# Score blocks of a head packed into fewer PSUM banks, and the projection tiles of the next heads dealt out one by one, in a one-core encoder block on Trainium2

## The chip, the cores and the metric

The kernel runs as one program on one core of a Trainium2 chip. TensorE (PE) multiplies matrices, VectorE (DVE) and ScalarE (ACT) read its results and work on tiles, GpSimd (POOL) takes element-wise work between SBUF tiles, and SyncE (SP) issues most DMAs. PE writes into PSUM, which this kernel uses as eight banks of 128 x 512 fp32; everything else lives in SBUF. The metric is the device time of one execution, in microseconds (us), lower is better. Before the change the median of three runs is 889.13 us (888.93 to 891.29).

## The reference, cut to what matters

One layer over 512 frames of 1024 features, batch 1. What the change touches is the attention branch:

```python
u = einsum('bsd,de->bse', rmsnorm(h, norm_mix_g), w_in)       # q | k | v | rnn_x | rnn_gate | gate_A | gate_B
ya = chunked_band_attention(q, k, v, rel_table) @ w_attn_out  # 16 heads x 64, chunks of 64, key band of 9 chunks
yb = (rg_lru(causal_depthwise_conv(xr)) * gelu(gr)) @ w_rnn_out
h  = h + (sigmoid(ga) * ya + sigmoid(gb) * yb) @ w_o
h  = h + (silu(g) * up) @ w_ffn_out                           # FFN of 2816, on rmsnorm(h)
return rmsnorm(h, final_norm_g)
```

With 512 frames the band is just the causal mask by chunks, so a head has four query blocks of 128 rows whose scores are 128, 256, 384 and 512 keys wide.

## The kernel before, in words

All weights and activations are fp32 and are split into a high and a low part (`split`, L78: ACT copies the high part, DVE subtracts it to get the low part); a product is three matmuls, high x high, high x low and low x high (`mm3`, L72). The profile therefore names PE work by L74, L75 and L76, which are the lines of that helper, and splits by L80 (ACT) and L81 (DVE).

The stages, in order of time: normalise and transpose x; the RNN branch's projections, gates and scan; the products with `w_rnn_out` (`po_yb`); 16 attention heads; the products with `w_attn_out` (`po_ya`), `w_o`, then the FFN and the final norm. The attention stage is the one that the change rewrites.

Within it PE's order is written out by hand (`manual_schedule` for PE, L720): the loop of L721 emits for each head h

1. `transposed(h)` (L660): ten 128 x 128 transposes of the normalised probabilities `p` into three PSUM tiles `pT`, the third of them of the `mm` kind; each is split by ACT and DVE into `pp`;
2. `scores(h+1)` (L638): for each of the four query blocks two matmuls (L650, L651) into a PSUM tile `s`; then DVE adds the bias and takes the row maximum (L653, the maximum is called `m`), ACT takes the exponential (L654), DVE the reciprocal `rl` of the row sums (L655) and POOL multiplies (L657, four pieces a head);
3. the tiles that `laid(h)` (L700) puts before the product: projections that later heads need. `q_tile` and `k_tile` (L593, L604) make queries and keys of a pair of heads, 24 matmuls of 512 columns each; `v_tile` (L627) makes values of four heads for 128 frames, 24 matmuls of 256 columns; in the last four heads `gate` (L560) makes gate tiles `po_ga`;
4. `weigh(h)` (L677): the product `o` with the values, eight matmuls;
5. the tiles that `laid(h)` puts behind it.

The order of the other engines' instructions is made by a scheduler from the same program.

PSUM is dealt out by tags (L69): four banks `mm`, two `s`, two `t`. In this stage `t` belongs to the first two tiles of `pT`, `s` to the scores of query blocks 0 and 1, and `mm` to everything else: the third `pT`, the scores of blocks 2 and 3, every q, k, v and gate tile, and `o`. A PE matmul that opens a tile waits until the readers of the bank's last tile are done.

The copies of a k tile are many (L604): for each of its two heads ACT writes the high part (L611), DVE the low part (L612), ACT copies the high part to the other half of the partitions (L613), and POOL copies the low part there (L614).

Weights come through `prefetch` (L217) in the order of `plan` (L94): SP loads a `raw` tile (three buffers), ACT and DVE split it into `whl` (four buffers). `weights(name)` loads ahead by one planned chunk. The tiles `rnn` and, later, `aT` (the attention output, split) share four large buffers of the tag `big`.

Of the kernel before, what the change touches and what calls it, by code (L numbers as in the profile page):

```python
# [36 lines left out]
def block_kernel(ctx: ExitStack, tc: tile.TileContext, x, norm_mix_g, w_in, b_merge, rel_table,  # L37
# [23 lines left out]
    z_stack, zp = opened("z", 1, "right")  # L61
# [7 lines left out]
    def mm_tile(name, tag="mm"):  # L69
        return ps.tile([P, S], F32, tag=tag, bufs=4 if tag == "mm" else 2, name=name)  # L70
# [37 lines left out]
    def plan_v(gr):  # L108
        plan(f"v{gr}", cols(w_in, C_V + gr * CW))
# [4 lines left out]
        plan(f"yb{j}", cols(w_rnn_out, j * P))  # L114
    for pr in range(1, HEADS // 2):
        plan_qk(pr)
        if pr in (2, 4, 6):
            plan_v(pr // 2)
    for j in (4, 6):
        plan(f"ga{j}", cols(w_in, C_GA + j * P))  # L120
    for j in range(0, KT, 2):
# [11 lines left out]
    whole, every = slice(0, CW), slice(0, S)  # L133
    raws = {}
    extra = {}

    def load(name, k):
        _, parts, rows, kts = chunks[index[name]]
# [78 lines left out]
    def prefetch(n):  # L217
        while len(made) < min(n, len(chunks), index.get(barrier[0], len(chunks))):
            name, parts, rows, kts = chunks[len(made)]
            if name in strassen:  # L220
                made.append(weight_sums(name))
                continue
            tiles = []
            wide = sum(width for *_, width in parts)
            step = 4 * CW // wide
            for k in range(0, kts, step):
                n_ = min(step, kts - k)
                if name in extra:
                    hl = extra[name].tile([P, 2, n_, wide], F32R, tag="whl", bufs=4, name=f"whl_{name}_{k}")
                else:  # L230
                    hl = wp.tile([P, 2, n_, wide], F32R, tag="whl", bufs=4, name=f"whl_{name}_{k}")
                if (name, k) not in raws:
                    load(name, k)
                raw = raws.pop((name, k))
                if len(made) == 0 and k:
                    act.activation(hl[:, 0], raw[:], AF.Copy)
                    pool.tensor_sub(hl[:, 1], raw[:], f(hl[:, 0]))
                else:
                    split(hl[:, 0], hl[:, 1], raw[:])
                tiles.append(hl)  # L240
            made.append(lambda part, k, at, tiles=tiles, step=step: tiles[k // step][:, part, k % step, at])
# [312 lines left out]
        return po  # L554


    zs = [[zp.tile([P, 2, S], F32, name=f"z{w}{j}") for j in range(0, KT, 2)] for w in "ab"]
    ta, zB = ([t[j // 2][:, j % 2] for j in range(KT)] for t in zs)

    def gate(w, j):  # L560
        po = tile_of(f"g{'ab'[w]}{j - j % 2}", j % 2)
        act.activation((ta, zB)[w][j], po[:], AF.Tanh, bias=hb[:, 16 + 8 * w + j:17 + 8 * w + j], scale=0.5)
# [30 lines left out]
    def q_tile(pr):  # L593
        po = mm_tile(f"po_q{pr}")
        project(po, weights(f"qk{pr}"), 0, xnT)
        q = qk_pool(pr).tile([P, 2, S], F32R, tag="qk", bufs=3, name=f"q{pr}")
        for e in range(2):
            own, other = halves(e)
            src = backwards(po[own, :])
            act.activation(blocks(q[own, e]), src, AF.Copy, scale=0.125)  # L600
            dve.scalar_tensor_tensor(blocks(q[other, e]), src, 0.125, blocks(f(q[own, e])), ALU.mult, ALU.subtract)
        qk[pr] = [q]

    def k_tile(pr):  # L604
        po = mm_tile(f"po_k{pr}")
        project(po, weights(f"qk{pr}"), 1, xnT)
        kh = qk_pool(pr).tile([P, 2, S], F32R, tag="qk", bufs=3, name=f"kh{pr}")
        kl = qk_pool(pr).tile([P, 2, S], F32R, tag="qk", bufs=3, name=f"kl{pr}")
        for e in range(2):
            own, other = halves(e)  # L610
            act.activation(kh[own, e], po[own, :], AF.Copy)  # L611
            dve.tensor_sub(kl[own, e], po[own, :], f(kh[own, e]))  # L612
            act.activation(kh[other, e], po[own, :], AF.Copy)  # L613
            pool.tensor_copy(kl[other, e], kl[own, e])  # L614
        qk[pr] += [kh, kl]
# [11 lines left out]
    def v_tile(gr, t):  # L627
        wv = weights(f"v{gr}")
        po = mm_tile(f"po_v{gr}_{t}", "mm" if gr else "t")
        for k in range(KT):  # L630
            mm3(po[:, 0:256], xnT[k][:, 0, t * P:(t + 1) * P], xnT[k][:, 1, t * P:(t + 1) * P],
                wv(0, k, whole), wv(1, k, whole), k == 0, k == KT - 1)
        v = aw.tile([P, 2, 4, HD], F32R, tag="v", bufs=8, name=f"v{gr}_{t}")
        split(v[:, :, 0::3], v[:, :, 1:3], po[:, 0:256].rearrange("p (a b d) -> p a b d", a=2, b=2))
        vs.setdefault(gr, []).append(v)


    def scores(h):  # L638
        pr, e = divmod(h, 2)
        q, kh, kl = qk[pr]  # L640
        bias = bias_tile(h)
        lsum = cp.tile([P, NT], F32, tag="lsum", bufs=2, name=f"l{h}")
        nmax = cp.tile([P, NT], F32, tag="nmax", bufs=2, name=f"m{h}")
        rl = cp.tile([P, NT], F32, tag="rl", bufs=2, name=f"rl{h}")
        prob = [aw2.tile([P, (qb + 1) * P], F32, tag=f"p{qb}", name=f"p{h}_{qb}") for qb in range(NT)]
        for qb in range(NT):
            w = (qb + 1) * P
            sc = mm_tile(f"s{h}_{qb}") if qb >= 2 else ps.tile([P, S], F32, tag="s", bufs=2, name=f"s{h}_{qb}")
            qs = q[:, e, qb * P:(qb + 1) * P]
            pe.matmul(sc[:, 0:w], qs, kh[:, e, 0:w], start=True, stop=False)  # L650
            pe.matmul(sc[:, 0:w], qs, kl[:, e, 0:w], start=False, stop=True)  # L651

            dve.tensor_tensor_reduce(prob[qb][:], sc[:, 0:w], bias[:, S - w:S], -1.0, 3e38, ALU.add, ALU.min, nmax[:, qb:qb + 1])  # L653
            act.activation(prob[qb][:], prob[qb][:], AF.Exp, bias=nmax[:, qb:qb + 1], scale=-1.0, accum_out=lsum[:, qb:qb + 1])  # L654
        dve.reciprocal(rl[:], lsum[:])  # L655
        for qb in range(NT):
            pool.tensor_scalar(prob[qb][:], prob[qb][:], rl[:, qb:qb + 1], 1.0, ALU.mult, ALU.mult)  # L657
        return prob
# [39 lines left out]


    def laid(h):  # L700
        m, at = divmod(h, 4)
        qs, ks, va = (lambda pr: lambda: q_tile(pr)), (lambda pr: lambda: k_tile(pr)), (lambda t: lambda: v_tile(m + 1, t))
        if h >= 12:
            return [lambda: gate(0, h - 8)], []
        first_, second = 2 * m + 2, 2 * m + 3
        return {0: (([qs(1), ks(1)] if m == 0 else []) + ([] if m == 0 else [qs(first_)]), [qs(first_)] if m == 0 else []),
                1: ([ks(first_)], [va(0)]),
                2: ([va(1), va(2)], [va(3)]),
                3: ([qs(second)], [ks(second)])}[at]

    for t in range(NT):
        v_tile(0, t)
# [274 lines left out]
```

## Time and profile before

| what | value |
|---|---|
| median of three runs | 889.13 us |
| the three runs | 889.13, 891.29, 888.93 us |
| span of the profiled execution, first to last instruction | 887.1 us |
| PE busy in the span | 870.7 us, 98% |
| DVE busy in the span | 551.2 us, 62% |
| ACT busy in the span | 470.8 us, 53% |
| POOL busy in the span | 105.3 us, 12% |
| attention stage, first transpose to first `po_ya` | 247.53 to 443.93 us |
| PE busy from 247 to 444 us | 191.60 of 197.00 us |

The profiled execution's own time is known only as its span, 887.1 us; the median of the runs lies 2.0 us above it, which is what lies around the first and the last instruction.

How to read it: a busy engine is one with an instruction running, and matmuls overlap, so PE's busy share alone does not tell where it loses time. The useful view in this kernel is the list of PE instructions in order of time: the distance from one start to the next is what a matmul costs the stream, and a longer distance is a wait. A bracket at the end of such a row gives the idle time before it and the instruction that ended it. "<-" reads "out from in" when it stands between tiles and "waited for" when it stands between instructions.

### The profile page before, as it was taken

Reading aid. Unit: us, or ns where it says so; the run is one execution under the profiler, and the core shown is the slowest. Engines: PE = TensorE matmul, PEld = TensorE weight load, DVE = VectorE, ACT = ScalarE, POOL = GpSimd, SP = SyncE. Lnnn points to the kernel's source line nnn. Section 1 sums busy time; section 2 is a strip of 40 time slices with the busy share of each in tenths; the row PEclk is TensorE's granted clock in tenths of the full one; section 3 lists DMA queues with packets and bytes.
Section 4 is the critical chain, followed back from the end, with each engine's and each line's share of the span. In section 5 each row is a group of like instructions: output and inputs, shape, how many; then the busy total and the mean of one; then the engine's idle time right before and its main releaser. Section 6 shows DMA issues by size and latency. Waiting matters only on the chain.

```text
span 887.1 us, 13322 instructions
## 1 busy us (share of the span) xinstructions
PE 870.7 (98%) x5220; PEld 775.2 (87%) x5220; DVE 551.2 (62%) x856; ACT 470.8 (53%) x823; POOL 105.3 (12%) x141
## 2 busy tenths in 40 slices
PE   8999999999999999999999999999999999999997
PEld 5988888888888889797888889999999999888886
DVE  6776557563456576675556556888878887553203
ACT  7566646652256575666633465656555555723103
POOL 4012111120112131212200000000000001300100
PEclk9999999999999999999999999999999999999999
DMA  8323223333333232232123720524333332353002
GB/s 266 90 77 110 82 94 95 120 95 95 107 91 88 81 98 73 72 108 72 48 96 117 263 67 30 162 77 123 116 95 96 99 126 86 120 181 123 28 1 96
DMA packets 86080, 90.11 MB, mean 102 GB/s; under 512 B 5376, under 2 KB 74608, under 8 KB 86016
## 3 DMA queue, kind: packets, MB, share of 16 engines
q1 hardware_dynamic: 84640, 85.78, 31.0%
q10 hardware_dynamic: 1376, 3.47, 1.0%
q8 instruction: 41, 0.67, 0.3%
q14 instruction: 23, 0.19, 0.1%
HBM read 87.10 MB, written 2.14 MB: 101 GB/s over the span
## 4 chain that ended last, share of the span: by engine, by line
PE 95%; DVE 2%; ACT 1%; DMA 1%; issue 0%; ACTq 0%; DVEq 0%
PE po_out L75 5%; PE po_out L76 5%; PE po_out L74 5%; PE p_fg L74 2%; PE o L688 2%; PE p_fg L76 2%; PE p_fu L76 2%; PE p_fu L75 2%; PE p_fg L75 2%; PE p_fu L74 2%; PE po_v L74 2%; PE po_ga L74 2%; PE po_v L76 2%; PE po_v L75 2%; PE po_q L74 2%; PE po_k L74 2%
## 5 line engine op out<-in xcount | busy, mean ns | idle before, releaser
L75 PE MATMUL po_out<-whl_fo,act_hi 128*128 128x512 f32 (+1 forms) x198 | 72.5, 366 | 0.0
L74 PE MATMUL po_out<-whl_fo,act_hi 128*128 128x512 f32 (+1 forms) x198 | 72.3, 366 | 0.0
L76 PE MATMUL po_out<-whl_fo,act_lo 128*128 128x512 f32 (+1 forms) x198 | 71.7, 365 | 0.0
L81 DVE TENSOR_TENSOR whl_fo<-raw_fo,whl_fo 128x1024 fp32r<-128x1024 f32 x22 | 27.8, 1273 | 44.3 <-ACT whl_fo L80 43.7
L657 POOL TENSOR_SCALAR p<-p,rl 128x128 f32<-128x128 f32 (+1 forms) x64 | 35.8, 577 | 138.6 <-DVE rl L655 138.3
L871 POOL TENSOR_TENSOR act_lo<-act,act_hi 128x1024 fp32r<-128x1024 f32 x4 | 10.9, 2718 | 323.9 <-ACT act_hi L870 321.9
L80 ACT ACTIVATE whl_fo<-raw_fo 128x1024 fp32r<-128x1024 f32 x22 | 23.0, 1057 | 49.0 <-PE po_out L76 35.2
L74 PEld LDWEIGHTS po_out<-whl_fo,act_hi 128*128 128x128 f32 x198 | 37.4, 189 | 6.0
L75 PEld LDWEIGHTS po_out<-whl_fo,act_hi 128*128 128x128 f32 x198 | 37.4, 189 | 6.0
L76 PEld LDWEIGHTS po_out<-whl_fo,act_lo 128*128 128x128 f32 x198 | 37.3, 189 | 5.9
L654 ACT ACTIVATE p<-p,m 128x128 f32<-128x128 f32 (+1 forms) x64 | 35.8, 562 | 11.1 <-DVE m L653 10.7
L74 PE MATMUL po_v<-whl_v,xnT 128*128 128x256 f32 x128 | 36.5, 285 | 0.0
L76 PE MATMUL po_v<-whl_v,xnT 128*128 128x256 f32 x128 | 36.2, 283 | 0.0
L75 PE MATMUL po_v<-whl_v,xnT 128*128 128x256 f32 x128 | 36.2, 283 | 0.0
L653 DVE CUSTOM_DVE_ANT_0 p<-s,bias 128x128 f32<-128x128 f32 (+1 forms) x64 | 29.7, 484 | 0.7 <-issue 0.5
L81 DVE TENSOR_TENSOR whl_qk<-raw_qk,whl_qk 128x1024 fp32r<-128x1024 f32 x16 | 20.9, 1308 | 14.3 <-ACT whl_qk L80 14.3
L75 PE MATMUL po_xr<-xnT,whl_xr 128*128 128x512 f32 (+1 forms) x80 | 27.9, 354 | 0.6 <-DVE xnT L358 0.5
L74 PE MATMUL po_q<-xnT,whl_qk 128*128 128x512 f32 x64 | 25.3, 395 | 2.7 <-DVE m L653 2.7
L81 DVE TENSOR_TENSOR whl_fg_s<-s_fg,whl_fg_s 128x1024 fp32r<-128x1024 f32 x20 | 25.6, 1294 | 3.7 <-ACT whl_fg_s L80 3.7
L81 DVE TENSOR_TENSOR pp<-pT,pp 128x384 fp32r<-128x384 f32 (+1 forms) x48 | 27.9, 596 | 0.0
L74 PE MATMUL po_gr<-xnT,whl_gr 128*128 128x512 f32 (+1 forms) x80 | 27.8, 349 | 0.1
L76 PE MATMUL po_gr<-xnT,whl_gr 128*128 128x512 f32 (+1 forms) x80 | 27.5, 348 | 0.3 <-DVE whl_gr L81 0.3
(347 smaller groups left out, 3044.7 us busy)
## 6 DMA issues: line engine op xcount, KB each, us to landing
raw_fg<-in_w_ffn_in_dram SPq DMA_DIRECT2D x24, 512.0 KB, 4.4
raw_fu<-in_w_ffn_in_dram SPq DMA_DIRECT2D x22, 512.0 KB, 3.9
raw_fo<-in_w_ffn_out_dram SPq DMA_DIRECT2D x22, 512.0 KB, 4.6
raw_qk<-in_w_in_dram SPq DMA_DIRECT2D x32, 256.0 KB, 3.2
raw_xr<-in_w_in_dram SPq DMA_DIRECT2D x8, 512.0 KB, 4.5
raw_gr<-in_w_in_dram SPq DMA_DIRECT2D x8, 512.0 KB, 3.5
raw_ga<-in_w_in_dram SPq DMA_DIRECT2D x8, 512.0 KB, 3.5
raw_gb<-in_w_in_dram SPq DMA_DIRECT2D x8, 512.0 KB, 3.6
```

The source lines that it names most:

```text
L74: pe.matmul(o, sh, mh, start=start, stop=False, skip_group_check=parts)
L75: pe.matmul(o, sh, ml, start=False, stop=False, skip_group_check=parts)
L76: pe.matmul(o, sl, mh, start=False, stop=stop, skip_group_check=parts)
L80: act.activation(hi, src, AF.Copy)
L81: dve.tensor_sub(lo, src, f(hi))
L653: dve.tensor_tensor_reduce(prob[qb][:], sc[:, 0:w], bias[:, S - w:S], -1.0, 3e38, ALU.add, ALU.min, nmax[:, qb:qb + 1])
L654: act.activation(prob[qb][:], prob[qb][:], AF.Exp, bias=nmax[:, qb:qb + 1], scale=-1.0, accum_out=lsum[:, qb:qb + 1])
L657: pool.tensor_scalar(prob[qb][:], prob[qb][:], rl[:, qb:qb + 1], 1.0, ALU.mult, ALU.mult)
L688: pe.matmul(po[:, S - n:S], st, pp[i][:, part, lo:lo + n], start=kb == 0 and part == 0, stop=kb == NT - 1 and part == 1)
L871: (pool if i in (0, 1, 2, 4) else dve).tensor_sub(lo[:], o[:], f(hi[:]))
```

## The change

Two things are changed, both in the attention stage; the number and the shapes of the matmuls stay what they were.

**Banks.** A head's scores of query blocks 0 and 1 (128 and 256 columns) now go into one bank of the tag `s`, side by side; those of block 2 (384 columns) into the other `s` bank; only those of block 3 (512 columns) still take an `mm` bank. A head takes one `mm` bank less for its scores. In the program all eight matmuls now stand before the four DVE instructions.

**Dealing of tiles.** `laid` now gives each of the heads 1 to 11 exactly one tile of queries or keys before the product and one tile of values behind it. Odd heads make queries (of pair 1 + (h+1)/2), even heads keys (of pair 1 + h/2); head 0 makes queries and keys of pair 1 and one values tile; head 12 makes the last keys (pair 7) before its product and the first of the four late gate tiles behind it; heads 13 to 15 make a gate tile before their product, as they did. Before, the tiles came in groups of four heads: in such a group PE's order was, behind the scores, q and o (first head; head 0 has q, k, o, q); k, o, v; v, v, o, v; q, o, k.

**Buffers.** Values weights are planned one pair earlier, and their split tiles get buffers of their own instead of the common `whl` ones (`homes`): five of the six in the large `big` buffers, the sixth in a tile `late`, which afterwards holds the four late gate tiles (`za_late`).

```diff
@@ plan @@
-        if pr in (2, 4, 6):
-            plan_v(pr // 2)
+        if pr in (1, 3, 5):
+            plan_v((pr + 1) // 2)
@@ prefetch @@
-                if name in extra:
+                if (name, k) in homes:
+                    pl, tag, bufs = homes[name, k]
+                    hl = pl.tile([P, 2, n_, wide], F32R, tag=tag, bufs=bufs, name=f"whl_{name}_{k}")
+                elif name in extra:
@@ gates @@
-    zs = [[zp.tile([P, 2, S], F32, name=f"z{w}{j}") for j in range(0, KT, 2)] for w in "ab"]
-    ta, zB = ([t[j // 2][:, j % 2] for j in range(KT)] for t in zs)
+    zs = [[zp.tile([P, 2, S], F32, name=f"z{w}{j}") for j in range(0, KT // (1 + (w == "a")), 2)] for w in "ab"]
+    ta, zB = ([t[j // 2][:, j % 2] for j in range(2 * len(t))] for t in zs)
+    for gr in (1, 2, 3):
+        for k in (0, 4):
+            homes[f"v{gr}", k] = (zp, "late", 1) if (gr, k) == (3, 4) else (rnp, "big", 4)
@@ scores @@
+        banks = [ps.tile([P, S], F32, tag="s", bufs=2, name=f"s{h}_{i}") for i in range(2)] + [mm_tile(f"s{h}_2")]
+        scs = [banks[0][:, 0:P], banks[0][:, P:3 * P], banks[1][:, 0:3 * P], banks[2][:]]
         for qb in range(NT):
             w = (qb + 1) * P
-            sc = mm_tile(f"s{h}_{qb}") if qb >= 2 else ps.tile([P, S], F32, tag="s", bufs=2, name=f"s{h}_{qb}")
             qs = q[:, e, qb * P:(qb + 1) * P]
-            pe.matmul(sc[:, 0:w], qs, kh[:, e, 0:w], start=True, stop=False)
-            pe.matmul(sc[:, 0:w], qs, kl[:, e, 0:w], start=False, stop=True)
-            dve.tensor_tensor_reduce(prob[qb][:], sc[:, 0:w], bias[:, S - w:S], -1.0, 3e38, ALU.add, ALU.min, nmax[:, qb:qb + 1])
+            pe.matmul(scs[qb], qs, kh[:, e, 0:w], start=True, stop=False)
+            pe.matmul(scs[qb], qs, kl[:, e, 0:w], start=False, stop=True)
+        for qb in range(NT):
+            w = (qb + 1) * P
+            dve.tensor_tensor_reduce(prob[qb][:], scs[qb], bias[:, S - w:S], -1.0, 3e38, ALU.add, ALU.min, nmax[:, qb:qb + 1])
@@ laid @@
-        m, at = divmod(h, 4)
...
-        return {0: (([qs(1), ks(1)] if m == 0 else []) + ([] if m == 0 else [qs(first_)]), [qs(first_)] if m == 0 else []),
-                1: ([ks(first_)], [va(0)]),
-                2: ([va(1), va(2)], [va(3)]),
-                3: ([qs(second)], [ks(second)])}[at]
+        before, after = [], []
+        if h == 0:
+            before += [lambda: q_tile(1), lambda: k_tile(1)]
+        elif h < 13:
+            before.append(lambda: (q_tile if h % 2 else k_tile)(1 + (h + 1) // 2 if h % 2 else 1 + h // 2))
+        if h < 12:
+            after.append(lambda: v_tile(1 + h // 4, h % 4))
+        if h == 12:
+            late = zp.tile([P, 2, 2, S], F32, tag="late", bufs=1, name="za_late")
+            ta.extend(late[:, i, c] for i in range(2) for c in range(2))
+            after.append(lambda: gate(0, 4))
+        elif h > 12:
+            before.append(lambda: gate(0, h - 8))
+        return before, after
```

The order in which each engine's instructions stand changes with it, from the first scores of the stage to its last. Three places are shown, all around the scores of head 5, which PE emits in head 4. The number behind a name is that of a buffer; `s5_0` is the first score tile of head 5.

PE, the scores of head 5 and the first matmul behind them, before:

```order
L650 MATMUL s5_0_2751<-kh2_2355,q2_2268 128x128
L651 MATMUL s5_0_2751<-kl2_2356,q2_2268 128x128
L650 MATMUL s5_1_2756<-kh2_2355,q2_2268 128x256
L651 MATMUL s5_1_2756<-kl2_2356,q2_2268 128x256
L650 MATMUL s5_2_2761<-kh2_2355,q2_2268 128x384
L651 MATMUL s5_2_2761<-kl2_2356,q2_2268 128x384
L650 MATMUL s5_3_2766<-kh2_2355,q2_2268 128x512
L651 MATMUL s5_3_2766<-kl2_2356,q2_2268 128x512
L74 MATMUL po_q4_2776<-xnT_158,whl_qk4_0_2630 128x512
```

and now:

```order
L658 MATMUL s5_0_2707<-kh2_2488,q2_2360 128x128
L659 MATMUL s5_0_2707<-kl2_2489,q2_2360 128x128
L658 MATMUL s5_0_2707<-kh2_2488,q2_2360 128x256
L659 MATMUL s5_0_2707<-kl2_2489,q2_2360 128x256
L658 MATMUL s5_1_2708<-kh2_2488,q2_2360 128x384
L659 MATMUL s5_1_2708<-kl2_2489,q2_2360 128x384
L658 MATMUL s5_2_2709<-kh2_2488,q2_2360 128x512
L659 MATMUL s5_2_2709<-kl2_2489,q2_2360 128x512
L74 MATMUL po_k3_2731<-xnT_158,whl_qk3_0_2324 128x512
```

Four score tiles have become three, and the tile behind them is now the keys of pair 3 instead of the queries of pair 4. In the program before, `po_q4` was given the bank of `s5_2`; now no tile of the stage between the heads 1 and 12 is opened in a bank that scores of the same head's step have just left: a queries tile takes the bank of an earlier values or keys tile, a keys tile that of an earlier queries tile.

DVE, among the maxima of head 5, before (`whl_v2_4` is the low half of a weight split, `pp4_0` that of a transposed tile):

```order
L653 ISA p5_1_2748,m5_2745<-s5_1_2756,bias5_2741 128x256
L653 ISA m5_2745 128x1
L81 TENSOR_TENSOR whl_v2_4_2782<-raw_v2_4_2783,whl_v2_4_2782 128x1024
L653 ISA p5_2_2749,m5_2745<-s5_2_2761,bias5_2741 128x384
L653 ISA m5_2745 128x1
L81 TENSOR_TENSOR pp4_0_2719<-pT4_0_2722,pp4_0_2719 128x512
```

and now, from the last third of the transposed tiles on:

```order
L81 TENSOR_TENSOR pp4_2_2677<-pT4_2_2691,pp4_2_2677 128x384
L662 ISA p5_2_2705,m5_2701<-s5_1_2708,bias5_2697 128x384
L662 ISA m5_2701 128x1
L662 ISA p5_3_2706,m5_2701<-s5_2_2709,bias5_2697 128x512
L662 ISA m5_2701 128x1
L81 TENSOR_TENSOR whl_qk5_0_2875<-raw_qk5_0_2876,whl_qk5_0_2875 128x1024
L664 RECIPROCAL rl5_2702<-l5_2700 128x4
L619 TENSOR_TENSOR kl3_2757<-po_k3_2731,kh3_2756 64x512
```

The split of a weight tile has moved from between the maxima to behind them, and the split of the keys comes behind the reciprocal.

POOL, around the multiplications of head 5, before:

```order
L614 COPY kl3_2710<-kl3_2710 64x512 x2
L657 TENSOR_SCALAR p5_0_2747<-p5_0_2747,rl5_2746 128x128
L657 TENSOR_SCALAR p5_1_2748<-p5_1_2748,rl5_2746 128x256
L657 TENSOR_SCALAR p5_2_2749<-p5_2_2749,rl5_2746 128x384
L657 TENSOR_SCALAR p5_3_2750<-p5_3_2750,rl5_2746 128x512
```

and now:

```order
L666 TENSOR_SCALAR p5_0_2703<-p5_0_2703,rl5_2702 128x128
L666 TENSOR_SCALAR p5_1_2704<-p5_1_2704,rl5_2702 128x256
L666 TENSOR_SCALAR p5_2_2705<-p5_2_2705,rl5_2702 128x384
L666 TENSOR_SCALAR p5_3_2706<-p5_3_2706,rl5_2702 128x512
L621 COPY kl3_2757<-kl3_2757 64x512 x2
```

The two copies of the keys of pair 3 now stand behind the four multiplications. Of these keys the scores of head 6 are made, which PE now reaches one product, one values tile and ten transposes after the keys tile; before, a whole head lay between.

More of the change, by code (lines that the diff above doesn't have):

```diff
@@ L135, in block_kernel @@
     extra = {}
+    homes = {}
     def load(name, k):
@@ L700, in laid @@
     def laid(h):
-        m, at = divmod(h, 4)
[L702 to L705, printed above, removed]
-        return {0: (([qs(1), ks(1)] if m == 0 else []) + ([] if m == 0 else [qs(first_)]), [qs(first_)] if m == 0 else []),
-                1: ([ks(first_)], [va(0)]),
-                2: ([va(1), va(2)], [va(3)]),
-                3: ([qs(second)], [ks(second)])}[at]
+        before, after = [], []
[12 more added lines that the diff above has]
+        return before, after
     for t in range(NT):
```

## The prediction

> **What bounds the kernel now.** I read the page first.
>
> ```profile
> span 887.1 us, 13322 instructions
> PE 870.7 (98%) x5220; PEld 775.2 (87%) x5220; DVE 551.2 (62%) x856; ACT 470.8 (53%) x823; POOL 105.3 (12%) x141
> PEclk9999999999999999999999999999999999999999
> ```
>
> PE is busy 98% of the span at full granted clock: time goes away only where PE's stream has a hole or where work is taken from it, and this change takes none. So the second view is who PE waited for; these are its longest three rows and its one row for a weight (total us, times, longest).
>
> ```profile
> PE po_q L74 <- DVE m L653: 2.7, 2, 1.3
> PE po_ga L74 <- DVE m L653: 1.3, 1, 1.3
> PE po_k L74 <- DVE m L653: 1.2, 1, 1.2
> ...
> PE po_gr L76 <- DVE whl_gr L81: 0.3, 1, 0.3
> ```
>
> Four waits, all of a projection tile behind scores, all for DVE's row maximum, so all for a bank. The third view is PE in order of time (start, length, line, count) over heads 4 and 5:
>
> ```profile
> 310.00 0.40 PE L651 MATMUL s<-kl,q 128*128 128x512 f32 x1
> 311.74 0.50 PE L74 MATMUL po_q<-xnT,whl_qk 128*128 128x512 f32 x1 [1.34 <-DVE m L653]
> 317.33 1.37 PE L688 MATMUL o<-pp,v 128*128 128x512 f32 x8
> 319.57 0.31 PE L650 MATMUL s<-kh,q 128*128 128x128 f32 x1
> 320.70 0.40 PE L651 MATMUL s<-kl,q 128*128 128x512 f32 x1
> 320.94 0.39 PE L74 MATMUL po_k<-xnT,whl_qk 128*128 128x512 f32 x1
> 326.40 1.37 PE L688 MATMUL o<-pp,v 128*128 128x512 f32 x8
> 327.62 0.33 PE L74 MATMUL po_v<-whl_v,xnT 128*128 128x256 f32 x1
> 331.55 0.30 PE L650 MATMUL s<-kh,q 128*128 128x128 f32 x1
> 331.69 0.28 PE L651 MATMUL s<-kl,q 128*128 128x128 f32 x1
> 332.90 0.31 PE L74 MATMUL po_v<-whl_v,xnT 128*128 128x256 f32 x1
> ```
>
> By starts, the last score matmul costs 0.24 us when nothing is waited for (320.70 to 320.94) and 1.74 before `po_q4` (310.00 to 311.74): a hole of 1.50. The tile behind it takes 5.59 (to 317.33) instead of 5.46 (320.94 to 326.40), 0.13 more. The other holes:
>
> ```profile
> 269.67 0.40 PE L651 MATMUL s<-kl,q 128*128 128x512 f32 x1
> 271.32 0.50 PE L74 MATMUL po_k<-xnT,whl_qk 128*128 128x512 f32 x1 [1.25 <-DVE m L653]
> 361.28 0.50 PE L74 MATMUL po_q<-xnT,whl_qk 128*128 128x512 f32 x1 [1.35 <-DVE m L653]
> 410.81 0.50 PE L74 MATMUL po_ga<-xnT,whl_ga 128*128 128x512 f32 x1 [1.35 <-DVE m L653]
> 428.84 0.40 PE L651 MATMUL s<-kl,q 128*128 128x512 f32 x1
> 429.35 0.50 PE L74 MATMUL po_ga<-xnT,whl_ga 128*128 128x512 f32 x1
> ```
>
> The first is 1.65 - 0.24 = 1.41, the last 0.51 - 0.24 = 0.27; the middle two have an idle time like `po_q4`'s (1.35 and 1.34), so 1.51 each. Why the maximum is late is seen on DVE at the same place:
>
> ```profile
> 309.43 0.29 DVE L653 CUSTOM_DVE_ANT_0 p<-s,bias 128x128 f32<-128x128 f32 x1
> 309.99 1.22 DVE L81 TENSOR_TENSOR whl_v<-raw_v,whl_v 128x1024 fp32r<-128x1024 f32 x1
> 311.13 0.55 DVE L653 CUSTOM_DVE_ANT_0 p<-s,bias 128x384 f32<-128x384 f32 x1
> ```
>
> The 384-wide maximum stands behind a weight split of 1.22; it ends at 311.68 and PE goes on at 311.74. Head 4 brings PE little between two score rounds, and its tile sits in that maximum's bank.
>
> **The change part by part.** *Banks and dealing.* The 384-wide scores leave the `mm` banks, and behind them stands a tile in a bank left a good part of a head ago. The four holes go: 1.41 + 1.50 + 1.51 + 1.51 = 5.93. The fifth goes too: before, that gate tile sat in the bank of `o13`, now in that of the gate tile in front of `o13`. With 0.27 the holes come to 6.20. The slow start behind a hole, 0.13, goes five times, 0.65; as I have measured it here at one of five I take 0.5. Together 6.7. Regrouping changes no matmul. A head of the new kind (transposes, scores, q or k, `o`, one values tile) is already in the rows without a hole, 319.57 to 331.55, 11.98 us, so its seams have no price to be guessed.
>
> *What the regrouping brings near.* In even heads a keys tile is now followed by `o`, one values tile and ten transposes, and then by scores that read these keys; before, nearly a whole head more lay between. The same stretch on PE is in the rows of head 5, where those scores read older keys, so nobody waited; its copies show when they would have been ready:
>
> ```profile
> 324.92 3.01 POOL L657 TENSOR_SCALAR p<-p,rl 128x128 f32<-128x128 f32 x4 [7.33 <-DVE rl L655]
> 328.08 0.60 POOL L614 CAST kl<-kl 64x512 fp32r<-64x512 f32 x1
> 328.66 0.58 ACT L613 ACTIVATE kh<-po_k 64x512 fp32r<-64x512 f32 x1
> 330.54 1.25 PE L668 MATMUL pT<-ident,p 128*128 128x128 f32 x10
> 331.19 1.13 DVE L81 TENSOR_TENSOR aT<-oacc,aT 128x512 fp32r<-128x512 f32 x1
> 332.35 0.42 DVE L81 TENSOR_TENSOR v<-po_v,v 128x256 fp32r<-128x256 f32 x1
> ```
>
> Probabilities are done at 327.93 and transposed from 330.54: 2.6 us to spare. The low half of the keys is copied by 328.68, the high half by 329.24, and the scores start at 331.55: 2.3 us to spare at least. What DVE gets more in front of these maxima in an even head is `aT` and the v split, at most 1.13 + 0.42, and in heads 2, 4 and 8 a values-weight split of 1.22: 1.55, or 2.77. Were DVE never idle there, all copies would be that much later: 0.7 to spare in three heads, 0.5 us too late in the other three, 1.4 in all. DVE is busy 62%, so most of it falls into idle time; the bound from below is 0. I take 0.2, nearer to the heads without the weight split.
>
> *Queries tiles of odd heads* open in a bank that a values tile left (heads 1, 3, 7, 9, 11). In the rows above that split ends at 332.77, and the next tile starts at 332.90: 0.13 to spare, but with `aT`, 1.13, directly in front. Now `aT` falls into the next head, so I take 0. `po_q4` waits for the copies of keys instead, on ACT behind the split of a weight whose load SP issues only in that head: I allow 0.3, at worst one old hole of 1.5.
>
> *Score bank shared by blocks 0 and 1.* DVE's first maximum now waits for the 256-wide matmuls too, queued behind it are the other maxima and the transposed tiles' splits, and ACT's exponentials wait for it.
>
> ```profile
> 320.00 0.28 PE L651 MATMUL s<-kl,q 128*128 128x256 f32 x1
> 320.81 0.29 DVE L653 CUSTOM_DVE_ANT_0 p<-s,bias 128x128 f32<-128x128 f32 x1
> ```
>
> Even where it is early in the queue, the first maximum starts 0.53 after the last of these matmuls has ended (320.28). Price 0; its bound is the 0.26 by which the two matmuls are later, 15 times, 3.9, if DVE were never behind. [...]
>
> *Weights.* Values weights get own buffers, the number of splits and loads stays; SP moves loads past one another. PE's one wait for a weight in the view above is 0.3, in an earlier stage, so 0 with `po_q4`'s allowance above.
>
> *After the stage* PE's stream and its prefetch distances are the same; what is earlier here stays earlier to the end.
>
> **Sum.** 6.7 less 0.2 and 0.3 is 6.2: the profiled span 887.1 would become 880.9. The median of the runs, 889.13, lies 2.0 above this span; the same distance holds, so 889.13 - 6.2 = 882.9 us. A measurement here tells about 0.3%, 2.7 us, from no change. The main case reaches from a gain of 6.9 (all five slow starts) to one of 5.2 (`po_q4` and the even heads at half their bounds, 0.75 each): 882.2 to 883.9.
>
> **The rivals.** *Half the gain.* The even heads' chain is late by 0.4 to 0.7 in each of the six even heads, 2 to 12: 2.4 to 4.2 are lost of 6.7, which gives 884.8 to 886.6. For it: the bound of 0.5 in three heads. Against: the margins seen are over 2 us. [...]
>
> ```profile
> 315.33 2.06 POOL L657 TENSOR_SCALAR p<-p,rl 128x128 f32<-128x128 f32 x4
> 325.49 1.32 DVE L81 TENSOR_TENSOR whl_qk<-raw_qk,whl_qk 128x1024 fp32r<-128x1024 f32 x1 [0.77 <-ACT whl_qk L80]
> ```
>
> Beside a split of 1.32 the four multiplications took 3.01 instead of 2.06, 0.95 more, and that is within the rows that I count from. A second split under them would cost 0.95 again, in six heads at most 5.7, less the spare time.
>
> *The wait changes its name.* The queries tiles of the five odd heads wait for the values tile's split, as the stalled tiles did for the maximum. It decides from 0.13 of delay on; with a weight split of 1.22 in front as well it is 1.1 each, 5.5 of 6.7 lost, 887.9, no change (to 891 if two splits are in front of some). For it: the 0.13 above. Against: the `aT` that ate the rest is gone from there.
>
> *Slower: POOL becomes the bound.* The copies of the low keys stand behind four multiplications, and these behind the reciprocal, which stands behind a weight split on DVE. If they land over 1.1 us behind their scores in each of six even heads, the gain is gone; at 1.8 it is 10.8 lost against 6.7, 889.13 + 4.1 = 893.2. The matmul that reads them starts at 331.69, 3.0 behind the 328.68 seen, so it needs copies 4.8 us later than seen; the splits put in front make 2.77.
>
> That the holes stay as they were cannot be: those tiles no longer open in that bank.
>
> **How the numbers follow.** Main case 0.68, half the gain 0.14, renamed wait 0.12, slower 0.06. Faster by over 0.3% (under 886.5) takes the first two, 0.82; within 0.3% 0.12; slower 0.06. The range holds the first two cases: from 881.8, the best sum of 882.2 less twice the 0.2 by which the lowest run lies under the median, to 886.7.
>
> **What would show it.** Right: no PE wait for `m` over 0.3 in the stage; its length, 196.4 us between these two rows, down to about 190;
>
> ```profile
> 247.53 1.25 PE L668 MATMUL pT<-ident,p 128*128 128x128 f32 x10
> 443.93 0.44 PE L74 MATMUL po_ya<-aT,whl_ya 128*128 128x512 f32 x1
> ```
>
> a head of about 12.0 us, equal for heads 1 to 11. Wrong, step by step: waits of scores for `kl` or `kh` in even heads (first rival or third), of `po_q` for the v split (second), idle PE before transposes with POOL as the one waited for (third), a hole only before `po_q4` (the load). If all holes are gone and the time is not down by 5 us, the loss lies behind the stage and my last part is wrong.

## The result, and the profile after

| what | before | after |
|---|---|---|
| median of four runs, us | 889.46 (888.93 to 891.29) | 881.99 (881.82 to 882.9) |
| ratio to before, 95% interval | | 0.9919, 0.9906 to 0.9931 |
| span of the profiled execution, us | 887.1 | 880.2 |
| attention stage, first transpose to first `po_ya`, us | 196.40 | 189.54 |

The changed kernel is faster by 0.8%, more than the 0.3% by which the runs of the kernel before differ (888.93 to 891.29). The forecast was 882.9.

The first lines of the profile's page, as they were shown for the kernel before:

```profile
span 880.2 us, 13310 instructions
PE 869.7 (99%) x5220; PEld 776.3 (88%) x5220; DVE 546.7 (62%) x856; ACT 472.4 (54%) x823; POOL 111.2 (13%) x141
PEclk9999999999999999999999999999999999999999
```

PE's busy time is down by 1.0 us and its span by 6.9: most of what went is idle time. The list of what PE waited for is complete here (us in total, times, longest; idle times under 0.15 us are not in it):

```profile
PE busy L305 <- DVE eps_t L311: 1.2, 1, 1.2
PE po_xr L74 <- ACT xnT L361: 0.8, 2, 0.4
PE pt_mix L357 <- DVE xs_mix L349: 0.6, 1, 0.6
PE po_xr L75 <- DVE xnT L362: 0.6, 1, 0.6
PE p_fg L74 <- ACT keepa_fg L279: 0.5, 1, 0.5
PE po_ga L74 <- DVE sp_p L451: 0.3, 1, 0.3
PE po_gr L76 <- DVE whl_gr L81: 0.3, 1, 0.3
```

The four rows with the maximum `m` are gone, and nothing of the attention stage has come in their place: every tile named here belongs to an earlier or a later stage. From 247 to 437 us PE is now busy for 190.00 of 190.00 us; before, from 247 to 444, it was busy for 191.60 of 197.00. The stage's ends and one head in it, PE in order of time:

```profile
247.70 0.49 PE L677 MATMUL pT<-ident,p 128*128 128x128 f32 x3
...
303.14 0.40 PE L659 MATMUL s<-kl,q 128*128 128x512 f32 x1
303.37 0.40 PE L74 MATMUL po_k<-xnT,whl_qk 128*128 128x512 f32 x1
...
308.84 1.37 PE L697 MATMUL o<-pp,v 128*128 128x512 f32 x8
310.05 0.33 PE L74 MATMUL po_v<-whl_v,xnT 128*128 128x256 f32 x1
...
312.98 1.25 PE L677 MATMUL pT<-ident,p 128*128 128x128 f32 x10
313.99 0.30 PE L658 MATMUL s<-kh,q 128*128 128x128 f32 x1
314.13 0.28 PE L659 MATMUL s<-kl,q 128*128 128x128 f32 x1
...
437.24 0.44 PE L74 MATMUL po_ya<-aT,whl_ya 128*128 128x512 f32 x1
```

The last score matmul gives way to `po_k3` 0.23 us after its start (303.14 to 303.37), with no bracket; the tile takes 5.47. Every distance repeats from head to head: the scores start at 302.02, 313.99 and 325.95, and each of the heads 1 to 11 takes 11.96 to 11.97 us.

### The profile page after: what moved, and what is told of

The parts are those of the page before. It is cut to its first block, busy times and chain, and to the rows that moved or that the text cites. A ratio compares the mean times of both kernels' runs of the same rounds, so it can differ in the third digit from the quotient of the medians.

```text
span 880.2 us, 13310 instructions
## 1 busy us (share of the span) xinstructions
PE 869.7 (99%) x5220; PEld 776.3 (88%) x5220; DVE 546.7 (62%) x856; ACT 472.4 (54%) x823; POOL 111.2 (13%) x141
## 4 chain that ended last, share of the span: by engine, by line
PE 97%; DVE 1%; ACT 1%; issue 1%; DMA 0%; ACTq 0%
PE po_out L74 5%; PE po_out L76 5%; PE po_out L75 5%; PE p_fg L74 2%; PE o L697 2%; PE p_fg L76 2%; PE p_fu L76 2%; PE p_fu L75 2%; PE p_fg L75 2%; PE p_fu L74 2%; PE pT L677 2%; PE po_v L74 2%; PE po_v L76 2%; PE po_v L75 2%; PE po_ga L74 2%; PE po_q L74 2%
## 5 line engine op out<-in xcount | busy, mean ns | idle before, releaser
L666 POOL TENSOR_SCALAR p<-p,rl 128x128 f32<-128x128 f32 (+1 forms) x64 | 39.7, 638 | 128.8 <-DVE rl L664 128.5
L663 ACT ACTIVATE p<-p,m 128x128 f32<-128x128 f32 (+1 forms) x64 | 35.8, 560 | 16.1 <-DVE m L662 16.1
L74 PE MATMUL po_gr<-xnT,whl_gr 128*128 128x512 f32 (+1 forms) x80 | 27.8, 349 | 0.1
L76 PE MATMUL po_gr<-xnT,whl_gr 128*128 128x512 f32 (+1 forms) x80 | 27.5, 348 | 0.3 <-DVE whl_gr L81 0.3
L75 PE MATMUL po_gr<-xnT,whl_gr 128*128 128x512 f32 (+1 forms) x80 | 27.6, 347 | 0.0
```

The source lines that it names most:

```text
L74: pe.matmul(o, sh, mh, start=start, stop=False, skip_group_check=parts)
L75: pe.matmul(o, sh, ml, start=False, stop=False, skip_group_check=parts)
L76: pe.matmul(o, sl, mh, start=False, stop=stop, skip_group_check=parts)
```

## The experiments

The theory: the holes were waits for a bank that the 384-wide scores left late, because their maximum stood behind a weight split on DVE; any edit that keeps the tile behind the scores out of such a bank gets the time. Its rivals: the three short heads of the kernel before (4, 8 and 12, in which PE had one projection tile and a product only) were the limit and the bank only showed it; or both parts of the change are needed together. Each run below is compared with the kernel before on the same chip, whose median there was 889.24 us for the first four and 889.07 for the last two.

### The packed scores alone

The kernel before, with the score tiles of the changed one; dealing, plan and buffers as before.

```diff
+        banks = [ps.tile([P, S], F32, tag="s", bufs=2, name=f"s{h}_{i}") for i in range(2)] + [mm_tile(f"s{h}_2")]
+        scs = [banks[0][:, 0:P], banks[0][:, P:3 * P], banks[1][:, 0:3 * P], banks[2][:]]
...
-            sc = mm_tile(f"s{h}_{qb}") if qb >= 2 else ps.tile([P, S], F32, tag="s", bufs=2, name=f"s{h}_{qb}")
...
-            pe.matmul(sc[:, 0:w], qs, kh[:, e, 0:w], start=True, stop=False)
+            pe.matmul(scs[qb], qs, kh[:, e, 0:w], start=True, stop=False)
...
```

> The kernel before with the packed scores alone (its dealing of the projection tiles and its weight plan kept). Theory (the holes are waits for a bank that the 384-wide scores left late): no wait of PE for a maximum m is left behind scores, which takes 6.2 us of holes away; but heads 4, 8 and 12 keep only a queries tile and the product between scores and transposes, and there POOL's p ended at 317.39 in the run of before, so that transposes that come 1.5 us earlier (317.04 in place of 318.54) should wait up to about 0.4 us each for p. Forecast: 5 to 6.5 us less than before, ratio 0.9927 to 0.9944. Rival A (the short heads themselves are the limit, the bank only shows it): the holes of heads 4, 8 and 12 come back in full, 1.5 us each, in front of the transposes as waits for p, and only head 1's and the last one's go: 1.7 us less, ratio 0.998. Rival B (both parts are needed): same as before.

Measured: 883.72 us, ratio 0.9938 (0.9925 to 0.995), 5.5 us less. PE, and then DVE, around the scores of head 5, the place where the kernel before had its hole of 1.50:

```profile
308.69 0.40 PE L652 MATMUL s<-kl,q 128*128 128x512 f32 x1
308.93 0.40 PE L74 MATMUL po_q<-xnT,whl_qk 128*128 128x512 f32 x1
```

```profile
308.97 1.22 DVE L81 TENSOR_TENSOR whl_v<-raw_v,whl_v 128x1024 fp32r<-128x1024 f32 x1
310.11 0.55 DVE L655 CUSTOM_DVE_ANT_0 p<-s,bias 128x384 f32<-128x384 f32 x1
```

The weight split still stands in front of the 384-wide maximum, which is no earlier than before: it starts 1.42 us behind the start of the last score matmul (1.13 in the kernel before), and `po_q4` does not wait for it. So the bank was the cause, and the late maximum only through the bank. Behind the product of the same head a new, smaller wait appears, because the short head leaves POOL too little time:

```profile
315.61 0.51 PE L670 MATMUL pT<-ident,p 128*128 128x128 f32 x3
316.41 0.98 PE L670 MATMUL pT<-ident,p 128*128 128x128 f32 x7 [0.29 <-POOL p L659]
317.15 0.31 PE L651 MATMUL s<-kh,q 128*128 128x128 f32 x1
```

From the first transpose to the scores it is 1.54 us instead of 1.01. The same is there at 364.00 and 412.32 (1.54 and 1.58), so the three short heads give 1.6 us of the 6.2 back. The theory holds: its residue of about 0.4 a head came out at 0.5 to 0.6. The rival of the short heads, with 1.5 each, falls.

### The dealing alone

The changed kernel with the score tiles of before; so it has the new dealing together with the new plan and buffers.

```diff
-        banks = [ps.tile([P, S], F32, tag="s", bufs=2, name=f"s{h}_{i}") for i in range(2)] + [mm_tile(f"s{h}_2")]
-        scs = [banks[0][:, 0:P], banks[0][:, P:3 * P], banks[1][:, 0:3 * P], banks[2][:]]
...
+            sc = mm_tile(f"s{h}_{qb}") if qb >= 2 else ps.tile([P, S], F32, tag="s", bufs=2, name=f"s{h}_{qb}")
...
```

> The changed kernel with each head's four score tiles as they were before (two in small banks, two in the large ring), the new dealing kept. Theory (what counts is that no tile of PE asks for a bank whose reader stands late in DVE's queue, and the dealing alone does that too): the tile behind scores now takes the bank that the values tile of the head before left, whose split ended at 315.62 in head 5 of the changed kernel against a start of 315.34, so a hole of about 0.3 us in heads 3, 5 and 9, where DVE splits values weights ahead of it, and none elsewhere: 5.5 to 6.9 us less than before, ratio 0.9922 to 0.9938. Rival (the packing carries the gain): holes of about 1.5 us behind scores stay in several heads: at most 2 us less, ratio 0.998 or more.

Measured: 882.82 us, ratio 0.9926 (0.9912 to 0.9939), 6.4 us less. PE around the scores of head 6, and DVE at the same time:

```profile
315.02 0.40 PE L658 MATMUL s<-kl,q 128*128 128x512 f32 x1
315.65 0.51 PE L74 MATMUL po_q<-xnT,whl_qk 128*128 128x512 f32 x1 [0.23 <-DVE v L81]
```

```profile
313.47 1.67 DVE L81 TENSOR_TENSOR whl_v<-raw_v,whl_v 128x1024 fp32r<-128x1024 f32 x1
315.17 0.42 DVE L81 TENSOR_TENSOR v<-po_v,v 128x256 fp32r<-128x256 f32 x1
```

One hole of 0.40 (0.63 instead of 0.23 from start to start), of the kind that the second rival of the prediction had in mind: the queries tile waits for the split of a values tile, with a weight split in front. Forecast were three of 0.3; besides this one there is only a smaller one, 0.28, before a gate tile at 423.44. The rival that packing carries the gain falls.

Each part alone thus takes most of the gain, 5.5 and 6.4 us of 7.2 (0.0081 of 889): the parts are two ways of taking the same holes away, not two terms of a sum. What the second adds is small, and different on each side: dealing saves the packed kernel its 1.6 us in the short heads, packing saves the dealt one two short waits. The intervals of the three ratios overlap; it is the stage, 191.06, 190.41 and 189.54 us long in the three profiles (packed, dealt, both), and the waits in it, that tell them apart.

### The values weights at their old place in the plan

The changed kernel; the weights of a group of values are loaded and split one pair of heads later.

```diff
-        if pr in (1, 3, 5):
-            plan_v((pr + 1) // 2)
+        if pr in (2, 4, 6):
+            plan_v(pr // 2)
```

> The changed kernel with the values weights at their old place in the plan of weights (behind the second pair of queries and keys of each group, not behind the first). Theory (the weights are covered wherever they stand): a time within 0.5 us of the changed kernel, ratio to before 0.991 to 0.9925. Rival (the earlier loads are a needed part of the gain): the splits of the values weights come too late for the first values tile of a group or stand ahead of maxima, and PE waits for whl_v or m in heads 0, 4 and 8 by 1 us or more each: ratio 0.995 or more.

Measured: 882.22 us, ratio 0.9921 (0.9908 to 0.9933), as the changed kernel; its span, 880.2 us, and its stage, 189.54, are the same too.

The place in the plan is worth nothing; the weights are covered. Whether the values weights need buffers of their own at all was not tried. The argument for them, not shown by a run, is that in the four common buffers values weights that stay in use for four heads would keep out the queries and keys weights that are needed before those heads end.

### POOL's multiplications twice

The changed kernel with four more multiplications a head.

```diff
+        for qb in range(NT):
+            pool.tensor_scalar(prob[qb][:], prob[qb][:], 1.0, 1.0, ALU.mult, ALU.mult)
         return prob
```

> The changed kernel with four more POOL multiplications by 1 behind the four of each head (values unchanged): 2.05 us more POOL work in a head, or 3.02 where DVE splits weights beside it. Theory (POOL's slack ahead of the transposes is about 0.3 to 0.6 us in even heads, 2.8 us in odd ones): holes in front of the transposes of 1.4 to 2.7 us in the seven even heads that carry a keys tile, none or under 0.3 us in odd heads up to 11: 10 to 19 us more than the changed kernel. Rival A (POOL is bound in every head): about 2 to 3 us in each of 15 heads, 30 to 45 us more. Rival B (POOL is never late): under 2 us more.

Measured: 894.36 us (891.99 to 896.92), ratio 1.0056 (1.0036 to 1.0076), some 12 us more than the changed kernel. The size is within the forecast, the places are not: of the seven even heads with a keys tile only 2, 4 and 8 got a hole at their end, in front of the next head's transposes, of 1.9, 2.8 and 2.0 us (one of 2.1 is in front of the transposes of head 14, where only a gate tile stands ahead, and one of 0.3 in front of those of head 15). With smaller delays beside them the stage of the profiled execution is 199.16 us long, 9.6 more than in the changed kernel. So the agreement in size is partly luck: the forecast spread it over seven heads, and the two longer runs (894.36 and 896.92, against 891.99 for the profiled one) also had a lower mean granted clock, 0.994 and 0.992 against 0.998. The rivals, POOL bound in every head or never late, both fall. PE and POOL at the end of head 4:

```profile
314.82 0.70 PE L679 MATMUL pT<-ident,p 128*128 128x128 f32 x2
317.32 0.33 PE L679 MATMUL pT<-ident,p 128*128 128x128 f32 x1 [1.79 <-POOL p L668]
317.90 0.98 PE L679 MATMUL pT<-ident,p 128*128 128x128 f32 x7 [0.25 <-POOL p L668]
```

```profile
311.22 0.15 POOL L429 MEMSET bias<- 64x64 f32 x1 [10.48 <-DMA bias<-ext_d]
311.47 3.03 POOL L666 TENSOR_SCALAR p<-p,rl 128x128 f32<-128x128 f32 x4
```

And POOL of head 6, where the doubled work ended at 341.44, just in time for transposes at 341.56:

```profile
335.42 3.03 POOL L666 TENSOR_SCALAR p<-p,rl 128x128 f32<-128x128 f32 x4 [7.84 <-DVE rl L664]
...
339.01 2.43 POOL L668 TENSOR_SCALAR p<-p 128x256 f32<-128x256 f32 x3
```

From the start of a head's scores (303.77 and 330.61) to POOL's first multiplication it is 7.7 us in head 4 and 4.8 in head 6. Two things are late in head 4, and both are seen in the changed kernel as well. One is the reciprocal that POOL waits for: in heads 2, 4 and 8 it stands behind one more weight split on DVE, which itself waits 1.1 us for ACT. In the changed kernel it starts 6.55 us behind the start of the scores in head 4 (302.02) and 4.46 in head 6 (325.95):

```profile
307.42 1.22 DVE L81 TENSOR_TENSOR whl_qk<-raw_qk,whl_qk 128x1024 fp32r<-128x1024 f32 x1 [1.11 <-ACT whl_qk L80]
308.57 0.17 DVE L664 RECIPROCAL rl<-l 128x4 f32<-128x4 f32 x1
...
330.41 0.18 DVE L664 RECIPROCAL rl<-l 128x4 f32<-128x4 f32 x1 [0.88 <-ACT p L663]
```

The other is POOL's filling of a corner of the next bias, which stands in front of the multiplications in heads 2, 4 and 8 alone and waits for the transfer of that bias:

```profile
309.40 0.15 POOL L429 MEMSET bias<- 64x64 f32 x1 [11.67 <-DMA bias<-ext_d]
309.64 3.02 POOL L666 TENSOR_SCALAR p<-p,rl 128x128 f32<-128x128 f32 x4
```

These multiplications end at 312.66 and the transposes start at 312.98. The room is larger than this 0.32: by the program, the first transpose reads only the first of the four pieces, and the fourth, 0.33 later, is the first one to read the last piece. In the doubled run a transpose that had waited started 0.06 behind its piece. That leaves 0.58 us to spare in head 4, by the same count 0.69 in head 2 and 0.30 in head 8, and 3 or more in the other heads up to 12. The tightest places of the changed kernel are at the stage's end, 0.34 in front of the transposes of head 14 and 0.12 in front of those of head 15.

### The same without the wait for the bias

The kernel of the section before, with the bias loaded in two transfers that leave the corner out.

```diff
-        sp.dma_start(out=b[:], in_=band)
+        sp.dma_start(out=b[:, 0:448], in_=bass.AP(tensor=src.tensor, offset=src.offset, ap=[[1, P], [1, 448]]))
+        sp.dma_start(out=b[0:64, 448:512], in_=bass.AP(tensor=src.tensor, offset=src.offset + 448, ap=[[1, 64], [1, 64]]))
```

> The kernel with POOL's work doubled (values unchanged), and each head's bias loaded in two transfers that leave out the 64 by 64 corner which POOL then fills, so that the filling no longer waits for a transfer to land. In the run with doubled POOL work the holes stood only in heads 2, 4, 8 (1.9, 2.8 and 2.0 us) and 14; in head 4 of the changed kernel POOL began its multiplications at 309.64, 0.9 us behind the reciprocal, because the filling of the corner waited until 309.40 for the bias. Theory (two delays add up there: DVE's split of weights in front of the reciprocal, about 2 us against head 6, and the filling, 0.7 to 0.9 us): the holes of heads 2, 4 and 8 shrink by 0.7 to 0.9 us each and stay, about 2 to 2.7 us less in all; the median falls from 894.4 to about 892. Rival A (the transfer alone makes these heads late): their holes go, 6.5 us less. Rival B (the filling only stood in time that POOL had to wait anyway): no change.

Measured: 891.93 us (889.55 to 893.16), ratio 1.0026 (1.0016 to 1.0035); by the two ratios 2.7 us less than with the wait; the two runs with the least time of each kernel, at granted clocks of 0.999 and 0.998, are 2.4 apart (889.55 and 891.99). The holes at the ends of heads 2 and 8 fell from 1.9 and 2.0 to 1.3 each, by 0.6 and 0.7, a little under the forecast. POOL of head 4:

```profile
310.28 2.06 POOL L667 TENSOR_SCALAR p<-p,rl 128x128 f32<-128x128 f32 x4 [2.38 <-DVE rl L665]
```

The bracket now names the reciprocal: both delays are there, and the filling was the smaller. The multiplications, started earlier, also take 2.06 instead of 3.03, as those without a weight split beside them do (2.05 in head 5 of the changed kernel); the first two of the added ones take 1.63 instead of 0.67, which fits a split that now meets these. In head 4 the wait became shorter too: the fourth transpose, the first one that needs POOL's last piece, starts 2.51 us behind the first instead of 3.08. But the hole as a whole did not shrink in this execution, because PE's clock fell. PE's busy time and its granted clock (the third number from the end of a row) in two stretches:

```profile
313.29:316.70 3.41, 1.72 (x13) 1.00 0.52 153
316.71:320.11 3.40, 3.29 (x14) 0.50 0.55 157
```

Behind the pause PE ran at half its clock for 3.4 us, and the scores there took 2.22 us instead of 1.35. So the two runs agree with two delays that add up, 0.6 to 0.7 us of each wait being the filling's; but the difference of the medians is partly one of clocks.

### More work for DVE behind each values tile

The changed kernel with the low half of each values split done six times.

```diff
+        if gr:
+            for again in range(5):
+                dve.tensor_sub(v[:, :, 1:3], po[:, 0:256].rearrange("p (a b d) -> p a b d", a=2, b=2), f(v[:, :, 0::3]))
```

> The changed kernel with DVE's part of each values tile's split done five times more (values unchanged), about 0.35 us each, so 1.7 us more DVE work in each of twelve heads, between the values tile and the scores' maxima. Theory (DVE has room in a head, and behind scores only some queries tiles take the bank of a values tile, with 1.25 to 1.35 us to spare): holes of about 0.4 us behind scores in front of five queries tiles (heads 1, 3, 7, 9, 11), and of about 0.6 us in front of the transposes behind heads 2, 4 and 8, where POOL's multiplications follow a reciprocal that comes later: 2 to 5 us more than the changed kernel, of 20 us of added work. Rival A (the renamed wait: the split of the values tile stands at the edge): 1 us or more in front of most queries tiles and the softmax late in every head: 10 us or more. Rival B (DVE has room for all of it): under 1 us.

Measured: 882.18 us, ratio 0.9919 (0.9904 to 0.9933): nothing lost but 0.23 us once, at the transposes in front of the scores of head 6. The theory's 2 to 5 us were wrong, and the rival that DVE has room for all of it came true. DVE's time for it:

```profile
L644 DVE TENSOR_TENSOR v<-po_v,v 128x256 fp32r<-128x256 f32 x60 | 25.2, 419 | 0.8
```

Sixty instructions more, 19.4 us more of DVE's busy time (566.1 against 546.7), are there, but the scheduler dealt them out among the head's other DVE work (one stands at 309.09 in head 4, another at 316.41, half a head later), and no queries tile waited for them. So the run shows that DVE has room for 1.6 us more in a head, and does not show how near the first split itself is to its queries tile; that is left open, with the 0.40 of the dealing alone as the only such wait that was seen.

## Why the prediction was right

**The bound and the holes.** The four holes and the fifth, 6.20 by the starts of before, are gone, all of them, as predicted, and for the reason given: the run with the packed scores alone leaves the maximum late and loses the holes. The slow first tiles behind the holes were put at 0.5 of a possible 0.65. By the starts the five tiles took 5.57 or 5.59 us in the kernel before and take 5.47 in the others, 0.10 to 0.12 less each: 0.56 in all, so the cautious 0.5 was nearly right. Measured, the stage is 196.40 - 189.54 = 6.86 us shorter; the holes and these tiles make 6.8 of it, and the rest, about 0.1, is in the seams between tiles, which the new order changes a little.

**The dealing.** That a head of the new kind has no price of its own held: 11.98 was read from before, 11.96 to 11.97 came. The prediction did not say that the short heads would show up without the dealing, about half a microsecond each, nor that either part would have done on its own; it treated the two as one edit, and the sum was not hurt by that.

**Even heads' copies (0.2).** Not spent. The row of POOL's copies in head 4 of the changed kernel:

```profile
312.72 0.60 POOL L621 CAST kl<-kl 64x512 fp32r<-64x512 f32 x1
```

It ends at 313.32, and the matmul that reads it starts at 314.13: 0.81 to spare where the bound was 0.5 too late. What came nearer is not the copies but the multiplications in front of them, with the 0.30 to 0.69 us of heads 2, 4 and 8 worked out above. The prediction saw them 2.6 us clear, as they were in another head; it counted the splits that would come in front, and did not see that the filling of the next bias could stand in front of them and wait for a transfer.

**Queries tiles (0) and `po_q4` (0.3).** No wait at either. The last of the copies of `po_k3`, whose bank `po_q4` takes, ends on ACT at 314.66,

```profile
314.06 0.60 ACT L620 ACTIVATE kh<-po_k 64x512 fp32r<-64x512 f32 x1
```

and the tile starts at 315.34: 0.68 to spare.

**The shared bank (0), weights (0), behind the stage (unchanged).** The first maximum of head 5 starts at 304.12, 2.1 us behind the scores' start, and no PE wait follows from it. The run with the dealing alone has separate banks and so shows the price: there the first maximum starts 1.64 us behind the scores, but the reciprocal 6.55 in both kernels. For the scores of head 4 the reciprocal starts 4.84 behind them there and 5.05 with the shared bank; 0.2 us is the most that the shared bank costs the softmax in any head. Moving the values weights in the plan changed nothing. The span lost 6.9 and the stage 6.86, so nothing was given back behind it.

**The sum.** 6.7 less 0.5 of allowances was 6.2; 6.9 came in the span. The median of the runs fell by 7.5, and the ratio's interval holds 6.1 to 8.4, so 6.2 and 6.9 cannot be told apart by the runs; the span and the stage do. The forecast of the median, 882.9, is 0.9 above the measured 881.99. Half a microsecond of that is the two allowances, which were not needed, and 0.2 is the distance from the span to the median: taken as 2.0, it is 1.8 in the profiled execution (881.99 and 880.2); the rest is what the slow first tiles, the holes and the seams gave beyond their terms. The measured time lies below the best sum of the main case, 882.2, and only 0.2 above the lower end of the range, which had been widened there by the runs' scatter alone. So the mechanism was right, and it is partly luck that the range held.

**The rivals.** Half the gain and POOL as the bound needed the even heads' chain 0.4 to 1.8 us late; the copies were early by 0.8 and the multiplications by 0.30 or more, and the doubled POOL work shows what crossing that costs. The prediction's price for a split beside the multiplications, 0.95, was read from rows that add the four instructions up. Taken one by one, in head 4 of the changed kernel:

```profile
310.44 0.58 POOL L666 TENSOR_SCALAR p<-p,rl 128x384 f32<-128x384 f32 x1
311.00 1.65 POOL L666 TENSOR_SCALAR p<-p,rl 128x512 f32<-128x512 f32 x1
```

```profile
310.61 1.49 DVE L81 TENSOR_TENSOR whl_qk<-raw_qk,whl_qk 128x1024 fp32r<-128x1024 f32 x1 [0.26 <-ACT whl_qk L80]
```

The third multiplication was running when the split began, and it took its usual 0.58; the split took 1.49 instead of 1.22. The fourth began while the split ran, and it took 1.65 instead of the 0.69 that it takes alone, ending 0.6 behind the split. So here the one that came second took longer: the split by 0.27 us, with 0.41 of the third multiplication still to run at its start, the fourth multiplication by 0.96, with 1.10 of the split still to run. In all seven heads of the changed kernel in which a split ran beside the multiplications, one of the four alone was longer (1.55 to 1.65 us instead of 0.58 or 0.69), and the four took 0.96 to 1.05 more than 2.05. The price of 0.95 was right, and in the changed kernel it lay within the spare time. The wait under a new name came, once and at 0.40, only in the dealing without the packing.

## What to carry to other kernels

When an engine that is busy 98% of the time waits, look for the tile that it opens there and for who read that bank last: packing small results of one consumer into a bank, or putting another tile behind them, each removed the wait here without making the late reader any faster. Two edits that remove the same wait need not add up (5.5 and 6.4 us alone, 7.2 together), so test each alone before summing them. Before adding work on an engine that is mostly idle, look for the one place in which its chain is latest: POOL is 13% busy here and has 0.30 to 0.69 us to spare in three heads, and 0.12 in front of the last one. And look at instructions one by one where a row of the profile adds several up.

## What the runs showed of the hardware

Pauses of PE of about the same length cost different amounts behind them. With POOL's work doubled, PE stood at the end of head 4 for 1.79 and 0.25 us and went on at full clock; without the wait for the bias it stood for 0.59 and 1.22 and went on at 0.50 until about 320. Stretches around the two pauses, each row with its length, PE's busy time and, third from the end, the granted clock; first two of the run without the wait, then two with POOL's work doubled:

```profile
314.30:316.80 2.50, 0.71 (x5) 0.28 (x3) 2.26 (x3) 1.53 (x3) 2.38 (x3) 0.98 0.71 210
316.80:318.20 1.40, 1.38 (x7) 1.38 (x8) 0.18 (x1) 0.77 (x2) 0.61 (x1) 0.50 0.36 94
```

```profile
314.80:317.30 2.50, 0.68 (x3) 0.28 (x2) 2.42 (x3) 1.45 (x3) 2.35 (x4) 1.00 0.73 210
317.30:318.60 1.30, 1.03 (x7) 0.84 (x8) 0.04 (x1) 0.28 (x1) 1.15 (x2) 1.00 0.20 55
```

In the 2.50 us of the pause PE was busy for nearly the same time, 0.71 and 0.68, and only behind the first did the clock fall. In the run without the wait it was low once more: from 428 to 436 us its mean is 0.79, and the seven transposes at 429.38, behind another pause of 1.22, took 1.75 us, as those at 316.82 did, instead of the 0.98 at full clock. The 3.41 us in front of them, and then as much around the hole of 1.50 us of the kernel before:

```profile
425.93:429.34 3.41, 1.96 (x10) 1.00 0.48 154
```

```profile
308.65:312.06 3.41, 2.06 (x14) 1.00 0.52 154
```

So PE was busy for 1.72 (shown further up) and 1.96 of the 3.41 us in front of the two falls, and for 2.06 around the hole, behind which the clock stayed at 1.00 to the end of the stage. But the 3.41 us up to 317.90 with POOL's work doubled hold both of its idle times, 2.04 us, and so only 1.37 of work, less than either, and the clock stayed at 1.00 from 300 to 330 us. What sets the clock the runs thus do not show. The runs of these two kernels spread over 4.9 and 3.6 us, those of the changed kernel, which has no such pause, over 1.1; that this spread comes from such falls of the clock is likely, as the longer runs have the lower mean clock (0.992 in the longest and 0.998 in the shortest with POOL's work doubled, 0.993 and 0.999 without the wait), but only one execution of each was traced.

POOL's four multiplications take 2.05 us alone and 3.01 to 3.10 where one of them meets a weight split of DVE. That happens in seven heads of the changed kernel and in three of the kernel before, so that the 64 multiplications took 39.7 us in all instead of 35.8, for the same work.
